# A decoder step with Strassen products: decode states through ScalarE and an adding transfer, and all 16 K tiles by Strassen in the heads and first convolutions

## The chip, the cores and the metric

The program runs on one core of one Trainium2 chip. The engines are TensorE (PE, with its weight loads shown apart as PEld), VectorE (DVE), ScalarE (ACT), GpSimd (POOL) and SyncE (SP). POOL and SP issue most transfers, each in the order of its own queue. The metric is the time of one execution on the device in microseconds; lower is better.

## The reference, cut to what matters

Two layers of a decoder trunk run over 512 prompt tokens and 8 single-token samples, which share all weights; all data is float32.

```
h = rmsnorm(x, norm_g);  z = h @ w_in            # 2048 -> 8192
b_c, c_c, x_c, g_c, q, k, v, g_r = split(z)      # 8 parts of 1024
y_conv = b_c * conv3(c_c * x_c) * silu(g_c)
q, k = rope(q), rope(k) / 16                     # 4 heads of 256
S_new = gamma * S + k^T v;  o = q S_new          # a sample: one step on its own state S (256 x 256)
y_ret = groupnorm(o) * gn_g * silu(g_r)          # the prompt: the same by chunks, from S = 0
x = x + concat(y_conv, y_ret) @ w_out
x = x + sigmoid(x @ w_pg) * (p @ w_ple)
```

Behind the last layer stands an RMSNorm. The new states of all samples and heads are outputs, with the retention decay gamma_h = 1 - 2^(-5-h).

## The kernel before

Activations lie transposed, 128 features by T = 520 tokens in a slot; there are 16 K tiles of 128 and NSLOT slots that are handed out and given back in program order. Tokens are two halves of TH = 260 (LEFT, RIGHT). A product of float32 accuracy is three matmuls of 128 x 128 by 128 x 260: `mm3` (L247 to L249) multiplies the high part of the weights by the high and the low part of the activation, and the low part of the weights by the high part.

Weights come from DRAM by SP into a ring of raw tiles (`raw_ring`) and are split by `split_w`: ScalarE writes the high part (L229), VectorE subtracts it to get the low part (L230). High and low go into `split_ring`, a ring of SPLIT tiles in pieces of up to four tiles (512 columns); a piece is free again when TensorE has used it.

`pair` makes two output tiles at a time. With s = 0 it is `plain`. With s > 0 the first s K tiles go through `strassen`: the pair's weights (two output tiles by two halves of the s tiles) and the activations (two halves of the tiles by the two halves of the tokens) are 2 x 2 blocks, and seven sets of s/2 products do what eight would. Each set's weights are sums made by VectorE (`add`, L319, pieces of up to four tiles); the sums of activations are made once per operand. The other 16 - s tiles follow plainly, two weight pieces and four products a tile. With s < 16 a fourth PSUM bank `c` is used and copied out at the end. The tables HEADS, CONVS, OUT_ROWS and GATES give s for each pair.

A layer is: four retention heads (`retain`), each of four pairs (q, k, v, gate); eight convolution steps of two pairs each; eight pairs with w_out; eight with w_pg. The prompt's retention runs in steps (`later`, called by `aside`) beside the pairs of the next head.

The decode step for a head h and a sample b runs in calls of `sample()`. A call comes at the end of every head's pair, and one more in the middle of every second; in the convolutions one in the middle of each pair, but for the last. A call first steps the sample that was loaded by the call ahead, then loads the next one: the state (`sret`, 256 KB, into slot `st`) and a row of key and query for all partitions (`kq`, into slot `kb`), both by POOL. The step (`sample_step`, L774) decays the state on ScalarE (L776), adds key times value on VectorE (L780, two of 256 columns, `vs` holds the values), sends the new state off (L781) and takes the dot products with the query (L784, two of 256 columns with an accumulator read each).

The order on each engine is set by the framework's scheduler, which may move instructions ahead within what data allows, by priorities; `keep(...)` holds an instruction in program order. Each engine then works its queue strictly in that order: one that waits holds up all behind it.

Of the kernel before, what the change touches and what calls it, by code (L numbers as in the profile page):

```python
# [13 lines left out]
P = 128  # L14
# [15 lines left out]
NSLOT = 75  # L30
# [22 lines left out]
HEADS = [[0, 0, 0, 8] + [14] * 12, [0] + [14] * 15]  # L53
CONVS = [[14] * 2 + [16] * 13 + [14]] * 2
# [10 lines left out]
SPLIT = 60  # L65
# [126 lines left out]
def trunk_kernel(  # L192
# [368 lines left out]
    vec = const.tile([P, 160], F32, name="vec")  # L561
# [17 lines left out]

    def gam(h):  # L580
        return vec[:, 128 + h : 129 + h]
# [93 lines left out]
    for a, b in ((0, 1), (1, 4), (4, 8), (8, 12), (12, 16)):  # L675
        raws = []
        if b == 1:
            raw = raw_ring.get(4)
            DMA.dma_start(raw.rearrange("p (m n) -> p m n", n=P), wi[0, 0:4, :, :P].rearrange("m p n -> p m n"))
            S.dma_start(vec, vecs)  # L680
            x = get()
            for n in (LEFT, RIGHT):
                DMA.dma_start(x[:, n], xT[0, :, n])
            xs.append(x)
            w = split_w(raw)
            ws = [[t[:, P * m : P * m + P] for t in w] for m in range(4)]
        else:
            for i in range(4):
                raws.append(load(wi[0, i, :, P * a : P * b]))
                if i < b - a:  # L690
                    x = get()
                    DMA.dma_start(x, xT[a + i])
                    xs.append(x)
            ws = [split_w(raw) for raw in raws]
            raw_ring.put(*raws)
# [20 lines left out]
    for l in range(DEPTH):  # L716
# [51 lines left out]
        def sample_load(h, b):  # L768
            st, kb = get(), get()
            SIDE.dma_start(st[:, :512], sret[l, h, b])  # L770
            SIDE.dma_start(kb[:, :512], kq[l, h, b].rearrange("c d -> (c d)").partition_broadcast(P))  # L771
            return h, b, st, kb

        def sample_step(h, b, st, kb):  # L774

            keep(S.activation(st[:, :512], st[:, :512], AF.Identity, scale=gam(h)))  # L776
            k = kb[:, 256:512]
            for e in range(2):
                c = slice(256 * e, 256 * e + 256)
                keep(V.scalar_tensor_tensor(st[:, c], k, vs[:, h, e, b : b + 1], st[:, c], MUL, ADD))  # L780
            SIDE.dma_start(o_rets[l, h, b], st[:, :512])  # L781
            for e in range(2):
                c = slice(256 * e, 256 * e + 256)
                V.tensor_tensor_reduce(k, st[:, c], kb[:, :256], 1.0, 0.0, MUL, ADD, osum[:, e, h, b : b + 1])  # L784
            put(st, kb)

        loaded = []

        def sample():

            if loaded:
                sample_step(*loaded.pop(0))
# [24 lines left out]
        def retain(h):  # L817
# [29 lines left out]
            for e, z in enumerate(head(mt + 4)):  # L847
                t = z.slot if z.ps is None else copied(z.ps).slot
                V.scalar_tensor_tensor(vs[:, h, e, :], t[:, SEQ:T], 1.0 / 16, rb[:, SEQ:T], MUL, MUL)
# [227 lines left out]
        for j in range(CJ):  # L1077
# [23 lines left out]
            if j == CJ - 1:  # L1101
                while loaded or todo:
                    sample()
# [375 lines left out]
```

## Time and profile before

| | |
|---|---|
| time, 3 runs | 2167.03, 2167.06, 2169.21 us; median 2167.06 |
| span of the profiled execution, first to last instruction | 2167.3 us |
| TensorE busy | 2147.8 us, 17861 matmuls, granted clock 0.999 |
| VectorE busy | 1896.1 us, 3849 instructions |
| ScalarE busy | 1264.5 us, 2647 instructions |
| GpSimd busy | 430.6 us, 746 instructions |
| moved by transfers | 387.31 MB, 179 GB/s on the mean |

The profiled execution's span lies within the three times, so a sum against the span holds for the times too. A row of a group gives the line, engine, operation, the tiles out<-in with their shapes, the count, then the busy time, the mean duration, and the idle time just before with what ended it. The busy time counts overlapped stretches once, so busy time over count is what one more costs, and the mean is how long one takes.

### The profile page before, as it was taken

The page shows a single profiled execution, that of the slowest core. Times are in us where ns is not written, and L with a number is a line of the kernel's source. Part 1 is how long each engine was busy: PE and PEld are TensorE (multiplying, and loading weights), DVE is VectorE, ACT ScalarE, POOL GpSimd, SP SyncE. Part 2 cuts the span into 40 slices and gives each one's busy share as a digit, 9 for nine tenths or more (in the row PEclk, how much of TensorE's full clock was granted, in tenths as well). Part 3 has the DMA queues.
Part 4 walks back from the last instruction along what each step waited for, and adds up shares of the span by engine and source line. Part 5 has one row for each costly group of instructions (what it writes and reads, how often), then busy time and mean ns, then how long its engine had stood idle before and what let it go on. Part 6 is the DMA issues. An engine that isn't in the chain of part 4 may idle for free. (4 is left out here: it accounts for less than half of the span.)

```text
span 2167.3 us, 48178 instructions
## 1 busy us (share of the span) xinstructions
PE 2147.8 (99%) x17861; PEld 2142.1 (99%) x17861; DVE 1896.1 (87%) x3849; ACT 1264.5 (58%) x2647; POOL 430.6 (20%) x746
## 2 busy tenths in 40 slices
PE   9999999999999999999999999999999999999998
PEld 9999999999999999999999999999999999999998
DVE  8889988998999987987997988989999998879884
ACT  8656655565555655655765655565645555456565
POOL 2313222211001211200212222231111022011011
PEclk9999999999999999999999999999999999999999
DMA  8555565545543745645645566664464355566455
GB/s 288 171 175 197 181 217 184 178 157 175 158 129 118 238 156 187 215 154 160 215 144 175 172 213 191 189 209 170 151 182 149 120 158 202 176 207 200 128 164 198
DMA packets 182861, 387.31 MB, mean 179 GB/s; under 512 B 25888, under 2 KB 56352, under 8 KB 182624
## 3 DMA queue, kind: packets, MB, share of 16 engines
q1 hardware_dynamic: 128704, 212.98, 31.6%
q0 software_dynamic: 53056, 169.84, 23.8%
q8 instruction: 140, 2.29, 0.4%
q10 hardware_dynamic: 864, 1.39, 0.2%
q14 instruction: 97, 0.79, 0.1%
HBM read 318.96 MB, written 65.15 MB: 177 GB/s over the span
## 5 line engine op out<-in xcount | busy, mean ns | idle before, releaser
L247 PE MATMUL ps_g<-slot,split 128*128 128x260 f32 x5465 | 1531.6, 284 | 7.2 <-ACT slot L307 2.9
L248 PE MATMUL ps_g<-slot,split 128*128 128x260 f32 x5465 | 1534.3, 282 | 0.3 <-DVE slot L555 0.3
L249 PE MATMUL ps_g<-slot,split 128*128 128x260 f32 x5461 | 1519.9, 283 | 0.5 <-DVE split L230 0.5
L229 ACT ACTIVATE split<-raw 128x512 fp32r<-128x512 f32 (+2 forms) x1347 | 777.3, 596 | 583.1 <-DVE raw L319 213.2
L247 PEld LDWEIGHTS ps_g<-slot,split 128*128 128x128 f32 x5465 | 1024.0, 188 | 10.1 <-ACT slot L307 3.7
L248 PEld LDWEIGHTS ps_g<-slot,split 128*128 128x128 f32 x5465 | 1028.5, 188 | 0.5 <-DVE slot L555 0.5
L249 PEld LDWEIGHTS ps_g<-slot,split 128*128 128x128 f32 x5461 | 1019.8, 188 | 1.0 <-DVE split L230 1.0
L230 DVE TENSOR_TENSOR split<-raw,split 128x512 fp32r<-128x512 f32 (+2 forms) x1346 | 849.2, 652 | 172.5 <-PE ps_g L248 85.4
L319 DVE TENSOR_TENSOR raw<-raw 128x512 f32<-128x512 f32 (+1 forms) x660 | 428.9, 660 | 32.5 <-DMA raw<-wi 23.7
L307 ACT ACTIVATE slot<-ps_g 128x260 f32<-128x260 f32 x336 | 127.4, 381 | 140.6 <-PE ps_g L249 122.7
L551 ACT ACTIVATE slot<-slot 128x520 fp32r<-128x520 f32 (+1 forms) x212 | 109.2, 562 | 46.6 <-DVE slot L414 11.1
L552 DVE TENSOR_TENSOR slot<-slot,slot 128x520 fp32r<-128x520 f32 (+1 forms) x212 | 124.4, 620 | 4.1 <-ACT slot L551 3.9
L781 POOL DMA_DIRECT2D o_rets<-slot x64 | 35.3, 552 | 351.6 <-DVE slot L780 131.7
L307 DVE TENSOR_TENSOR slot<-ps_g,slot 128x260 f32<-128x260 f32 x168 | 70.9, 424 | 6.0 <-PE ps_g L249 3.7
L869 POOL DMA_DIRECT2D slot<-hs x64 | 46.2, 724 | 118.7 <-DVE split L230 42.7
L814 POOL DMA_DIRECT2D hs<-slot x64 | 35.6, 556 | 139.3 <-DVE slot L755 61.3
L780 DVE SCALAR_TENSOR_TENSOR slot<-slot,vs,slot 128x256 f32<-128x256 f32 x128 | 56.1, 481 | 4.5 <-ACT slot L776 4.3
L746 DVE TENSOR_TENSOR slot<-slot,slot 128x520 f32<-128x520 f32 x80 | 55.8, 698 | 4.7 <-DMA o_rets<-slot 3.7
L770 POOL DMA_DIRECT2D slot<-sret x64 | 35.5, 554 | 114.6 <-ACT split L229 37.3
L1058 POOL DMA_DIRECT2D slot<-x1s x76 | 40.8, 538 | 87.6 <-PE ps_g L249 27.2
L1209 POOL DMA_DIRECT2D x2s<-slot x30 | 16.4, 545 | 201.6 <-DVE slot L1204 200.6
L771 POOL DMA_DIRECT2D slot<-kq x64 | 34.9, 547 | 106.0 <-DVE slot L876 22.2
(217 smaller groups left out, 1733.8 us busy)
## 6 DMA issues: line engine op xcount, KB each, us to landing
raw<-wi SPq DMA_DIRECT2D x377, 256.0 KB, 3.9
raw<-wo SPq DMA_DIRECT2D x128, 256.0 KB, 5.4
raw<-wg SPq DMA_DIRECT2D x122, 256.0 KB, 4.1
raw<-wi SPq DMA_DIRECT2D x136, 192.0 KB, 4.0
slot<-x1s POOLq DMA_DIRECT2D x76, 260.0 KB, 5.1
slot<-sret POOLq DMA_DIRECT2D x64, 256.0 KB, 4.0
hs<-slot POOLq DMA_DIRECT2D x64, 256.0 KB, 4.0
slot<-hs POOLq DMA_DIRECT2D x64, 256.0 KB, 5.2
```

What stands on the lines that cost most here:

```text
L229: S.activation(hi, raw, AF.Copy)
L230: V.tensor_tensor(lo, raw, F(hi), SUB)
L247: PE.matmul(out, wh, xh, start=start, stop=False, skip_group_check=more)
L248: PE.matmul(out, wh, xl, start=False, stop=False, skip_group_check=more)
L249: PE.matmul(out, wl, xh, start=False, stop=stop, skip_group_check=more)
L307: fn(*args)
L319: V.tensor_tensor(out[:, n], x[:, n], y[:, n], op)
L551: keep(S.activation(hi, src[:, n], AF.Copy))
L552: V.tensor_tensor(lo, src[:, n], F(hi), SUB)
L746: V.tensor_tensor(out[:, n], v, table[:, n], MUL)
L780: keep(V.scalar_tensor_tensor(st[:, c], k, vs[:, h, e, b : b + 1], st[:, c], MUL, ADD))
L869: SIDE.dma_start(t[:, :512].rearrange("p (m n) -> p m n", m=2), src)
```

## The change

The decode step is spread over three calls. A call steps one sample, prepares the next, and loads the key and query of the one after that. Preparing (`sample_add`) writes key times value into the state's slot on ScalarE, two instructions of 256 columns; then POOL sends the old state with `accum_op=ADD`, so that the transfer adds it to what lies there. The values in `vs` are divided by gamma, so the slot holds the new state over gamma. The step takes the dot products with GAMMA[h] as their scale, then ScalarE multiplies the state by GAMMA[h] and it is sent off. The dot products are now held in program order (`keep`), as is ScalarE's decay.

HEADS and CONVS go from 14 to 16 everywhere but in CONVS' last pair: 12 pairs of layer 0's heads, 15 of layer 1's, and the first two convolution pairs of each layer. NSLOT goes from 75 to 76, SPLIT from 60 to 56, and the constants `vec` from 160 to 128 columns.

```diff
-NSLOT = 75
+NSLOT = 76
...
+GAMMA = [1.0 - 2.0 ** (-5 - h) for h in range(H)]
+HEADS = [[0, 0, 0, 8] + [16] * 12, [0] + [16] * 15]
+CONVS = [[16] * 15 + [14]] * 2
-HEADS = [[0, 0, 0, 8] + [14] * 12, [0] + [14] * 15]
-CONVS = [[14] * 2 + [16] * 13 + [14]] * 2
...
-SPLIT = 60
+SPLIT = 56
...
         def sample_load(h, b):
-            st, kb = get(), get()
-            SIDE.dma_start(st[:, :512], sret[l, h, b])
+            kb = get()
             SIDE.dma_start(kb[:, :512], kq[l, h, b].rearrange("c d -> (c d)").partition_broadcast(P))
-            return h, b, st, kb
+            return h, b, kb
-        def sample_step(h, b, st, kb):
-            keep(S.activation(st[:, :512], st[:, :512], AF.Identity, scale=gam(h)))
-            k = kb[:, 256:512]
+        def sample_add(h, b, kb):
+            st = get()
             for e in range(2):
                 c = slice(256 * e, 256 * e + 256)
-                keep(V.scalar_tensor_tensor(st[:, c], k, vs[:, h, e, b : b + 1], st[:, c], MUL, ADD))
-            SIDE.dma_start(o_rets[l, h, b], st[:, :512])
+                keep(S.activation(st[:, c], kb[:, 256:512], AF.Copy, scale=vs[:, h, e, b : b + 1]))
+            SIDE.dma_start(st[:, :512], sret[l, h, b], accum_op=ADD)
+            return h, b, kb, st
+        def sample_step(h, b, kb, st):
             for e in range(2):
                 c = slice(256 * e, 256 * e + 256)
-                V.tensor_tensor_reduce(k, st[:, c], kb[:, :256], 1.0, 0.0, MUL, ADD, osum[:, e, h, b : b + 1])
+                keep(V.tensor_tensor_reduce(kb[:, 256:512], st[:, c], kb[:, :256], GAMMA[h], 0.0, MUL, ADD, osum[:, e, h, b : b + 1]))
+            keep(S.activation(st[:, :512], st[:, :512], AF.Copy, scale=GAMMA[h]))
+            SIDE.dma_start(o_rets[l, h, b], st[:, :512])
             put(st, kb)
-        loaded = []
+        loaded, added = [], []
         def sample():
+            if added:
+                sample_step(*added.pop(0))
             if loaded:
-                sample_step(*loaded.pop(0))
+                added.append(sample_add(*loaded.pop(0)))
             if todo:
                 loaded.append(sample_load(*todo.pop(0)))
...
-                V.scalar_tensor_tensor(vs[:, h, e, :], t[:, SEQ:T], 1.0 / 16, rb[:, SEQ:T], MUL, MUL)
+                V.scalar_tensor_tensor(vs[:, h, e, :], t[:, SEQ:T], 1.0 / 16 / GAMMA[h], rb[:, SEQ:T], MUL, MUL)
...
-                while loaded or todo:
+                while added or loaded or todo:
```

How this stands on the engines is shown at one call of `sample()`, the sixth, at the end of the pair for the second head's values in layer 0. Before, it steps the fifth sample of the first head; now it steps the fourth and prepares the fifth, which the next call steps, in the middle of the pair for the gate. Slots carry running numbers; what an instruction waits for stands in brackets (Activation is ScalarE, Pool GpSimd, DMASW a transfer of POOL's, DMAHW one of SP's). Lines of the new kernel are one to four off those of the old.

VectorE before: the fifth sample's two state updates (L780), then its dot products (L784) between weight splits (L230).

```order
L918 SCALAR_TENSOR_TENSOR slot_198_2369<-ps_kt,vec,slot_197_2368 128x256 [waits Activation_49]
L780 SCALAR_TENSOR_TENSOR slot_183_2055<-slot_184_2056,vs,slot_183_2055 128x256 [waits DMASW1_49,Activation_49]
L780 SCALAR_TENSOR_TENSOR slot_183_2055<-slot_184_2056,vs,slot_183_2055 128x256
L230 TENSOR_TENSOR split<-raw,split 128x512 [waits Activation_49]
L230 TENSOR_TENSOR split<-raw,split 128x512 [waits PE_49,Activation_49]
L784 ISA slot_184_2056,osum<-slot_183_2055,slot_184_2056 128x256 [waits DVE_49]
L784 ISA osum 128x1
L230 TENSOR_TENSOR split<-raw,split 128x256 [waits DMAHW4_49,PE_49,Activation_49]
L230 TENSOR_TENSOR split<-raw,split 128x256 [waits DMAHW6_49,Activation_49]
L784 ISA slot_184_2056,osum<-slot_183_2055,slot_184_2056 128x256 [waits DVE_49]
L784 ISA osum 128x1
L230 TENSOR_TENSOR split<-raw,split 128x384 [waits DMAHW2_49,PE_49,Activation_49]
```

VectorE after, from the second dot product of the fourth sample (L784, its accumulator read) to the first of the fifth, slot_199_2341:

```order
L784 ISA osum 128x1
L231 TENSOR_TENSOR split<-raw,split 128x512 [waits DMAHW6_49,PE_49,Activation_49]
L320 TENSOR_TENSOR raw<-raw 128x512 [waits DMAHW4_49,DVE_49]
L320 TENSOR_TENSOR raw<-raw 128x512 [waits DMAHW0_49,DVE_49]
L922 SCALAR_TENSOR_TENSOR slot_204_2494<-ps_vt,r5p,slot_203_2493 128x256 [waits DMASW4_49,Activation_49]
L231 TENSOR_TENSOR split<-raw,split 128x512 [waits DMAHW7_49,PE_49,Activation_49]
L231 TENSOR_TENSOR split<-raw,split 128x512 [waits PE_49,Activation_49]
L320 TENSOR_TENSOR raw<-raw 128x512 [waits DMAHW5_49,DVE_49]
L922 SCALAR_TENSOR_TENSOR slot_204_2494<-ps_vt,r5p,slot_203_2493 128x256 [waits Activation_49]
L308 TENSOR_TENSOR slot_202_2355<-ps_g,slot_202_2355 128x260 [waits DMASW6_49,Activation_49]
L320 TENSOR_TENSOR raw<-raw 128x512 [waits DVE_49]
L784 ISA slot_183_2029,osum<-slot_199_2341,slot_183_2029 128x256 [waits DMASW7_49]
```

The state updates are gone; the dot product of the fifth sample stands behind three splits (L231), four sums (L320) and three others, and waits for a transfer of POOL's.

ScalarE before, about the decay of the fifth sample (L776):

```order
L229 ACTIVATE split<-raw 128x384 [waits DMAHW6_49]
L917 ACTIVATE slot_197_2368<-ps_kt,vec 128x256 [waits DVE_49]
L776 ACTIVATE slot_183_2055<-slot_183_2055,vec 128x512 [waits DMASW0_49]
L229 ACTIVATE split<-raw 128x512 [waits DVE_49,Activation_49]
L229 ACTIVATE split<-raw 128x512 [waits DMAHW7_49,PE_49,Activation_49]
L229 ACTIVATE split<-raw 128x256 [waits DMAHW4_49,PE_49]
```

ScalarE after, from the decay of the fourth sample (L785, slot_182_2025) over the products of the fifth (L776) to the decay of the fifth:

```order
L785 ACTIVATE slot_182_2025<-slot_182_2025 128x512 [waits DMASW0_49,DVE_49]
L776 ACTIVATE slot_199_2341<-slot_183_2029,vs 128x256 [waits DMASW6_49]
L776 ACTIVATE slot_199_2341<-slot_183_2029,vs 128x256
L921 ACTIVATE slot_203_2493<-ps_vt,r5p 128x256 [waits PE_49]
L230 ACTIVATE split<-raw 128x512 [waits DMAHW7_49,PE_49]
L230 ACTIVATE split<-raw 128x512 [waits DVE_49,PE_49]
L921 ACTIVATE slot_203_2493<-ps_vt,r5p 128x256 [waits DVE_49]
L308 ACTIVATE slot_202_2355<-ps_g 128x260 [waits DMASW6_49,Activation_49]
L230 ACTIVATE split<-raw 128x512 [waits DMAHW3_49,PE_49]
L230 ACTIVATE split<-raw 128x512 [waits DVE_49,PE_49]
L785 ACTIVATE slot_199_2341<-slot_199_2341 128x512 [waits DMASW7_49,DVE_49,Activation_49]
```

The decay now waits for VectorE (its dot products), and the next sample's products stand right behind it, ahead of the next splits (L230).

POOL before: the sixth sample's state load (L770, slot_200_2382) stands four rows ahead of the fifth's new state going out (L781), and waits for nothing of the step.

```order
L770 DMA slot_200_2382<-sret 128x512 [waits PE_49]
L869 DMA slot_206_2526<-hs 128x2x256 [waits DMASW6_49,DMASW3_49]
L869 DMA slot_217_2960<-hs 128x2x256 [waits DMASW7_49,DVE_49,Pool_49]
L771 DMA slot_201_2383<-kq 128x512 [waits DMASW0_49,DVE_49]
L781 DMA o_rets<-slot_183_2055 128x512 [waits DMASW1_49,DVE_49,Activation_49]
L770 DMA slot_207_2560<-sret 128x512 [waits DMASW4_49,DMASW2_49,PE_49]
L781 DMA o_rets<-slot_200_2382 128x512 [waits DVE_49,Activation_49]
L771 DMA slot_208_2561<-kq 128x512 [waits DMASW3_49,DVE_49]
```

POOL after: the fifth sample's old state is sent (L777, slot_199_2341) right behind the fourth's new state (L786).

```order
L873 DMA slot_216_2899<-hs 128x2x256 [waits DMASW4_49,DVE_49,Pool_49]
L768 DMA slot_200_2345<-kq 128x512 [waits DMASW5_49,DVE_49]
L786 DMA o_rets<-slot_182_2025 128x512 [waits DMASW6_49,Activation_49]
L777 DMA slot_199_2341<-sret 128x512 [waits DMASW7_49,PE_49,Activation_49]
L786 DMA o_rets<-slot_199_2341 128x512 [waits DMASW0_49,Activation_49]
L777 DMA slot_206_2534<-sret 128x512 [waits DMASW2_49,PE_49,Activation_49]
L768 DMA slot_207_2538<-kq 128x512 [waits DMASW0_49,DVE_49]
```

A state's transfer stood some rows ahead of the step of the sample before it, and waited for its slot and for older transfers; now it stands behind that step's last transfer and waits for ScalarE's products too.

More of the change, by code (lines that the diff above doesn't have):

```diff
@@ L558, in split @@
         return op
-    vec = const.tile([P, 160], F32, name="vec")
+    vec = const.tile([P, P], F32, name="vec")
     def norm_g(l, k):
@@ L578, in kd @@
         return vec[:, c : c + 1]
-    def gam(h):
-        return vec[:, 128 + h : 129 + h]
     ident = const.tile([P, P], F32, name="ident")
@@ L679, in trunk_kernel @@
             DMA.dma_start(raw.rearrange("p (m n) -> p m n", n=P), wi[0, 0:4, :, :P].rearrange("m p n -> p m n"))
-            S.dma_start(vec, vecs)
+            S.dma_start(vec, vecs[:, :P])
             x = get()
```

## The prediction

> **What bounds the kernel now.** I read the page's busy table first, then the costliest groups, then the rate of matmuls in a quiet stretch. In the last row here the columns behind the stretch and its length are, for PE, the weight loads, DVE, ACT and POOL, the busy us and the number of instructions, then clock, DMA share and GB/s.
>
> ```profile
> span 2167.3 us, 48178 instructions
> PE 2147.8 (99%) x17861; PEld 2142.1 (99%) x17861; DVE 1896.1 (87%) x3849; ACT 1264.5 (58%) x2647; POOL 430.6 (20%) x746
> L247 PE MATMUL ps_g<-slot,split 128*128 128x260 f32 x5465 | 1531.6, 284 | 7.2 <-ACT slot L307 2.9
> 500.00:550.00 50.00, 50.00 (x420) 50.00 (x419) 44.04 (x89) 26.20 (x55) 8.75 (x15) 1.00 0.58 176
> ```
>
> TensorE is busy 99% of the span, and the costliest group shows 7.2 us of idle time in 1531.6. A group's "284 ns" overlaps its neighbours; what one matmul costs is the pace: 420 in 50 us, 119 ns each, at the full granted clock. The profiled execution's span is 2167.3 us; the three times given have the median 2167.06, so the sum below can be set against either.
>
> Where TensorE is not at that pace was read next, from its own waits and from stretches of 10 us (84 matmuls at full pace).
>
> ```profile
> PE ps_g L247 <- ACT slot L307: 2.9, 4, 1.3
> PE ps_g L247 <- ACT ps_g L307: 1.6, 2, 1.2
> PE ps_vt L913 <- DMA slot<-hs: 0.9, 1, 0.9
> ...
> 700.00:710.00 10.00, 8.80 (x73) 1.00 0.52 147
> 720.00:730.00 10.00, 7.88 (x64) 1.00 1.01 376
> 1780.00:1790.00 10.00, 8.71 (x73) 1.00 0.90 315
> 1790.00:1800.00 10.00, 9.44 (x79) 1.00 0.97 352
> ```
>
> The waits are small everywhere. The only sizable losses of pace are the two passages from the convolutions to w_out: 73, 64, 73 and 79 matmuls instead of 84 are 47 missing, 47 x 0.119 = 5.6 us, with the DMA engines at 0.52 to 1.01. So what shortens the program is fewer matmuls, as long as VectorE and ScalarE still deliver the split weights in time. How near VectorE is to its end shows by stage (the columns as above; the first four are layer 0's retention heads, then its convolutions, then two heads of layer 1):
>
> ```profile
> 87.00:168.00 81.00, 81.00 (x680) 81.00 (x679) 69.58 (x151) 46.89 (x101) 18.52 (x33) 1.00 0.57 188
> 168.00:253.40 85.40, 85.40 (x717) 85.40 (x716) 81.05 (x182) 51.47 (x115) 26.11 (x45) 1.00 0.63 199
> 253.40:346.30 92.90, 92.90 (x779) 92.90 (x778) 84.16 (x188) 55.37 (x123) 26.30 (x46) 1.00 0.66 207
> 346.30:410.00 63.70, 63.70 (x534) 63.63 (x533) 56.09 (x129) 38.53 (x87) 19.29 (x33) 1.00 0.55 178
> 410.00:700.00 290.00, 289.06 (x2415) 288.88 (x2414) 263.85 (x526) 158.92 (x320) 38.58 (x56) 1.00 0.48 149
> 1236.40:1322.90 86.50, 86.50 (x727) 86.50 (x727) 79.67 (x180) 51.85 (x116) 26.04 (x45) 1.00 0.62 195
> 1322.90:1417.70 94.80, 94.59 (x791) 94.39 (x791) 84.33 (x190) 55.49 (x124) 26.35 (x45) 1.00 0.65 199
> ```
>
> TensorE is busy to the last 0.01 us in the heads of layer 0, though VectorE works 81.05 of 85.40 us (95%) in one of them. That is the fact that I lean on most: the split ring is deep enough that a VectorE at 95% costs TensorE nothing.
>
> **TensorE's part of the change.** A pair of output tiles by s K tiles of Strassen takes 7s/2 + 4(16-s) products of three matmuls: 57 for s = 14, 56 for s = 16. Raised are 12 pairs of layer 0's heads, 15 of layer 1's, and two convolution pairs per layer: 31 pairs, 93 matmuls. 93 x 0.119 = 11.1 us off the path, the only term on it. [...]
>
> **VectorE's part.** Of the split groups, the pairs lose two pieces of 256 columns each (62), and seven splits and four sums of each grow from 384 to 512 (217 and 124). I price by busy time over count, since neighbours overlap.
>
> ```profile
> L230 DVE TENSOR_TENSOR split<-raw,split 128x512 fp32r<-128x512 f32 x1031 | 695.0, 690 | 147.8 <-PE ps_g L248 81.2 <-ACT split L229 51.8 <-issue 6.1
> L230 DVE TENSOR_TENSOR split<-raw,split 128x384 fp32r<-128x384 f32 x249 | 137.1, 555 | 16.2 <-ACT split L229 9.9 <-PE ps_g L248 3.4 <-ACT slot L551 1.9
> L230 DVE TENSOR_TENSOR split<-raw,split 128x256 fp32r<-128x256 f32 x66 | 27.3, 423 | 8.5 <-ACT split L229 7.6 <-PE ps_g L248 0.8
> L319 DVE TENSOR_TENSOR raw<-raw 128x512 f32<-128x512 f32 x520 | 354.1, 688 | 17.6 <-DMA raw<-wi 12.1 <-DMA raw<-wo 2.9
> L319 DVE TENSOR_TENSOR raw<-raw 128x384 f32<-128x384 f32 x140 | 77.4, 554 | 14.9 <-DMA raw<-wi 11.6 <-DMA raw<-wg 2.8
> L780 DVE SCALAR_TENSOR_TENSOR slot<-slot,vs,slot 128x256 f32<-128x256 f32 x128 | 56.1, 481 | 4.5 <-ACT slot L776 4.3
> ```
>
> One of 256 costs 0.414 us, so -62 x 0.414 = -25.6. A split grows from 137.1/249 = 0.551 to 695.0/1031 = 0.674: +217 x 0.123 = +26.8. A sum grows from 0.553 to 0.681: +124 x 0.128 = +15.9. That is +17.1 us, 0.55 a pair. The 128 state updates of the decode step leave: -56.1. Together -39 us; 1896 becomes about 1857. The dot products stay as they are, only their scale is another constant.
>
> **ScalarE's part.** It splits the same weights, saves one copy between banks in each of the 31 pairs (a fourth bank isn't used), and takes over the products of key and value.
>
> ```profile
> L229 ACT ACTIVATE split<-raw 128x512 fp32r<-128x512 f32 x1032 | 632.3, 626 | 462.3 <-DVE raw L319 188.2 <-PE ps_g L249 166.4 <-PE ps_g L248 45.1
> L229 ACT ACTIVATE split<-raw 128x384 fp32r<-128x384 f32 x249 | 127.2, 518 | 84.0 <-DVE raw L319 25.0 <-PE ps_g L248 24.2 <-PE ps_g L249 17.9
> L229 ACT ACTIVATE split<-raw 128x256 fp32r<-128x256 f32 x66 | 27.3, 415 | 36.7 <-DMA raw<-wi 29.0 <-PE ps_g L248 5.2 <-PE ps_g L249 1.9
> L307 ACT ACTIVATE ps_g<-ps_g 128x260 f32<-128x260 f32 x121 | 45.1, 373 | 16.4 <-PE ps_g L249 16.1
> L776 ACT ACTIVATE slot<-slot,vec 128x512 f32<-128x512 f32 x64 | 45.7, 714 | 0.0
> L917 ACT ACTIVATE slot<-ps_kt,vec 128x256 fp32r<-128x256 f32 x32 | 15.0, 468 | 9.2 <-DMA hs<-slot 3.2 <-DVE slot L918 2.5 <-PE ps_kt L913 2.2
> L874 ACT ACTIVATE slot<-slot 128x512 fp32r<-128x512 f32 x48 | 28.7, 624 | 10.1 <-DMA yc<-slot 4.6 <-DVE slot L904 2.4 <-DVE osum L784 2.1
> ```
>
> Splits: 217 x (0.613 - 0.511) - 62 x 0.414 = -3.5. Copies: -31 x 0.373 = -11.6. The 128 new products are 256 columns with a scale per partition, as in the row with ps_kt: 128 x 0.469 = +60.0. The 64 decays get a constant for a scale: 64 x (0.598 - 0.714) = -7.4. Together +37 us, 1264 to about 1302, 60% of the span: hidden, since no stage above has ScalarE over 61%. Were it not hidden, a head would show it as VectorE waiting for ScalarE's high halves.
>
> **The queues.** SP issues 62 transfers fewer for the same bytes (the two short pieces of each pair), worth nothing on the path. POOL issues as many as before, but the state's load now waits for ScalarE's products, and what stands behind it waits too: mostly the next kq row and the head's own fetches, needed a call later. The split ring shrinks from 60 to 56 tiles, 28 high and low pairs: 28 x 3 x 0.119 = 10.0 us of matmuls in stock instead of 10.7. I cost that at nothing; its cover is the stock itself. The 76th slot takes the room of those four tiles and of unused constants, and moves no work.
>
> **The new wait.** In the decode step a dot product now waits for a transfer that could not be sent before ScalarE wrote the products, and ScalarE writes them behind the decay of the sample ahead, which waits for that sample's dot products. So from one sample's dot products to the next one's there is a chain: decay, two products, transfer. All of VectorE's queue stands behind a dot product that waits, the weight splits above all, and TensorE behind those once the ring is empty. No row shows an adding transfer; the nearest is the plain load of the same 256 KB, whose 64 times from issue to landing (L770) are the first row.
>
> ```profile
> DMA to landing us min/median/max: 2.8/4.0/7.3
> ...
> L918 DVE SCALAR_TENSOR_TENSOR slot<-ps_vt,r5p,slot 128x256 fp32r<-128x256 f32 x32 | 15.4, 480 | 0.2 <-ACT slot L917 0.2
> L307 DVE TENSOR_TENSOR slot<-ps_g,slot 128x260 f32<-128x260 f32 x168 | 70.9, 424 | 6.0 <-PE ps_g L249 3.7 <-ACT slot L307 2.0
> ```
>
> By mean durations: 0.624 + 2 x 0.468 + 4.0 = 5.6 us if the adding transfer lands like the plain one. Against it stands the work that VectorE has between the two samples. At the place shown in the change's part it is three splits, four sums, two scaled subtractions (15.4/32 = 0.481) and one addition (70.9/168 = 0.422): 2.02 + 2.72 + 0.96 + 0.42 = 6.1 us. Added up so for all samples of a layer, five such gaps are 6.1 to 6.8 us (6.1, 6.1, 6.2, 6.8, 6.6), three 8.2 to 8.4, three 10.9 to 11.8, the others 13 and more. At 4.0 us nothing waits. The landing can hardly be shorter than the plain load's shortest, 2.8, which changes nothing, so the gain side of this term is zero. For the other end I double it, the state being read where it lands as well as where it comes from: 8.0, chain 9.6, and the dot products wait 16.2 us in the five gaps and 3.8 in the three, 20 us a layer. The idle time of VectorE in layer 0's four stretches of heads is 11.4 + 4.4 + 8.7 + 7.6 = 32.1 us; 20 samples fall there (20 x 2 x 0.438 = 17.5 us less work), 12 raised pairs (6.6 more) and 4.3 us less of TensorE's time leave 38.7. Twenty fit into 38.7, and one wait of 3.5 us is short against a stock of 10 us. I take the term as 0 on TensorE, nearer to the plain row, and keep 8 us as its upper end, from the second rival below.
>
> **Sum.** 2167.1 - 11.1 = 2156.0 us.
>
> **The rivals.**
> First, the adding transfer is so slow that the decode step's dot products stop VectorE: slower. It is decided where the waits of a layer pass the 38.7 us by half of 11.1 + 4.3 us, that is 46.4 us; with the gaps above that is a chain of 12.5, a landing of 10.9 us. At 12.0 us the waits are 52 + 8 = 60 us a layer, 21 more than the idle time, 43 for two layers: 2156 + 43 = 2199. [...] Against it: the plain load's longest landing of 64, with DMA shares of 0.57 to 0.66 around it, is 7.3 us. 7%.
> Second, the gain goes mostly back. With 8 us landing the close gaps come two by two: two waits of 3.5 us within 18 splits, whose 25 us of VectorE's work stand against 18 x 12 x 0.119 = 25.7 us of matmuls. VectorE falls 6 us behind there; if the ring is only half full, TensorE loses 1.3 us, three times a layer, and 8 us in all: 2164, no difference to be told. Against it is the 95% stretch. 12%.
> Third, the two passages lose less, as VectorE brings less backlog out of the convolutions (12 samples, 10.5 us less in 290): the 5.6 us go, 2150.5. Against it the DMA share of 1.01 in the worst stretch, which the change leaves. 15%.
> The forecast has the rest, 66%, with its own range of 2153 to 2159: 3 us either way for rearranged queues, about half of the passages' 5.6.
>
> **How the numbers follow.** A measurement of this kernel can tell a change from none at about 0.2%, 4.3 us. Faster: 66 + 15 = 81%; same, the second rival: 12%; slower, the first: 7%. The range leaves out the first rival and a part of the third: 2151 to 2164.
>
> **What will show it.** Right: TensorE's pace in the heads still 84 in 10 us with 93 matmuls fewer; VectorE's busy time near 1857, ScalarE's near 1302; the state's transfers landing within some 6 us, and hardly any idle time of VectorE before the dot products put down to them. Wrong: a row of VectorE's waits for the state's slot of tens of us, heads in which TensorE waits for split weights, a landing near 11 us, or a passage that loses clearly more than before.

## The result, and the profile after

The changed kernel takes 2202.4 us (2201.7 to 2203.1) where the kernel before takes 2167.5 in the same runs: 1.0161 times as long, interval 1.0147 to 1.0176. The forecast was 2156, with 2164 as its upper end. The first lines of the page, against those of before:

```profile
span 2201.0 us, 47885 instructions
PE 2152.6 (98%) x17768; PEld 2143.0 (97%) x17768; DVE 1877.6 (85%) x3659; ACT 1299.6 (59%) x2682; POOL 454.1 (21%) x746
```

The 93 matmuls are gone (17861 to 17768), and at the pace of 0.119 us a matmul that is 11.1 us. Two other things grew by more. TensorE's time without a matmul, span less busy time, was 2167.3 - 2147.8 = 19.5 us and is 2201.0 - 2152.6 = 48.4. Its busy time beyond the pace (called slow below), 2147.8 - 17861 x 0.119 = 22.3 before, is 2152.6 - 17768 x 0.119 = 38.2. So +28.9 idle, +15.9 slow, -11.1: together the 33.7 us between the two spans. What TensorE waited for, longest first, and what ScalarE's copies out of PSUM waited for:

```profile
PE ps_g L248 <- ACT slot L308: 17.4, 11, 3.9
PE ps_g L248 <- ACT split L230: 7.5, 6, 2.6
PE ps_g L250 <- DVE split L231: 3.7, 5, 1.7
```

```profile
ACT slot L308 <- DMA o_rets<-slot: 26.9, 12, 4.3
ACT slot L308 <- DMA hs<-slot: 6.3, 2, 3.5
```

L308 is the helper of `copy` and `plus` in `strassen`: ScalarE copies a bank into the pair's output slot, and TensorE cannot start the next product in that bank until it has. Before, such copies waited 2.8 us for `o_rets`; now 26.9. Most of the loss is in the retention heads (columns as in the prediction: PE, weight loads, VectorE, ScalarE, POOL, clock, DMA share, GB/s). The six stretches of heads held 4228 matmuls before and hold 3936 now; 292 at 0.119 us are 34.7 us of the 44.8. The convolutions run at full pace.

```profile
87.00:168.00 81.00, 79.06 (x650) 78.56 (x649) 71.36 (x137) 50.84 (x103) 17.82 (x27) 0.99 0.56 175
168.00:253.40 85.40, 84.38 (x698) 84.00 (x697) 73.14 (x149) 50.59 (x106) 24.23 (x40) 0.99 0.59 177
253.40:346.30 92.90, 86.99 (x704) 85.76 (x703) 74.67 (x154) 51.94 (x110) 28.19 (x45) 0.98 0.59 185
346.30:410.00 63.70, 61.26 (x506) 60.81 (x507) 55.33 (x113) 41.34 (x89) 19.23 (x31) 1.00 0.68 204
410.00:700.00 290.00, 290.00 (x2420) 290.00 (x2419) 262.26 (x510) 171.62 (x354) 45.30 (x69) 1.00 0.52 154
1236.40:1322.90 86.50, 80.50 (x654) 79.66 (x654) 69.33 (x141) 49.03 (x104) 24.48 (x40) 0.98 0.62 188
1322.90:1417.70 94.80, 89.29 (x724) 88.82 (x723) 79.07 (x163) 55.82 (x119) 27.31 (x44) 0.96 0.58 173
```

In the stretch at 253 us TensorE issues 704 matmuls where it issued 779, while VectorE is busy 75 of 93 us, less than before: no engine became the bound. One gap of it follows, first on ScalarE, then on POOL (start, duration, instruction, idle time before), then on TensorE by stretches (busy us and matmuls, clock, DMA share, GB/s):

```profile
254.96 0.62 ACT L785 ACTIVATE slot<-slot 128x512 f32<-128x512 f32 x1
...
259.17 0.63 ACT L230 ACTIVATE split<-raw 128x512 fp32r<-128x512 f32 x1 [1.40 <-PE ps_g L249]
264.06 0.67 ACT L308 ACTIVATE slot<-ps_g 128x260 f32<-128x260 f32 x2 [4.26 <-DMA o_rets<-slot]
```

```profile
255.58 2.14 POOL L873 DMA_DIRECT2D slot<-hs  x3 [3.17 <-ACT slot L785]
257.71 0.58 POOL L786 DMA_DIRECT2D o_rets<-slot  x1
```

```profile
258.00:261.00 3.00, 2.85 (x22) 1.00 0.76 210
261.00:265.00 4.00, 0.28 (x2) 1.00 1.06 347
265.00:268.00 3.00, 3.00 (x15) 0.50 0.49 162
268.00:271.00 3.00, 3.00 (x26) 0.94 0.00 0
```

The decay (L785), now the step's last work, ends at 255.6; the store of the new state is issued at 257.7, behind three fetches. The next pair's output has the same slot, so its copy stands still on ScalarE until 264.06, with the splits behind it, and TensorE has a gap of 3.72 us, from 261.06 to 264.78. Then the granted clock is 0.50 for 3 us, 15 matmuls where 25 fit. So the gap is paid nearly one and a half times. The clock record of the execution has six such stretches, each 3.41 us or twice that, 23.9 us in all; at half speed they lose 11.9 us, against 15.9 of slow time that came in. Before, there is none, but for one behind the last matmul, which both executions have. Ahead of the first of the six stands a gap of only 1.94 us, at 163.8.

### The profile page after: what moved, and what is told of

Read it like the earlier page. It is cut to its first block, busy times and chain, and to the rows that moved or that the text cites. A ratio compares the mean times of both kernels' runs of the same rounds, so it can differ in the third digit from the quotient of the medians.

```text
span 2201.0 us, 47885 instructions
## 1 busy us (share of the span) xinstructions
PE 2152.6 (98%) x17768; PEld 2143.0 (97%) x17768; DVE 1877.6 (85%) x3659; ACT 1299.6 (59%) x2682; POOL 454.1 (21%) x746
## 4 chain that ended last, share of the span: by engine, by line
PE 83%; DMA 6%; DVE 4%; issue 4%; ACT 2%; POOL 1%; SPq 0%; POOLq 0%; DVEq 0%; ACTq 0%
PE ps_g L248 26%; PE ps_g L250 26%; PE ps_g L249 26%; DMA raw<-wi 2%; DVE split L231 2%; DMA o_rets<-slot 1%; DMA hs<-slot 1%; DMA raw<-wo 1%; ACT split L230 1%; DMA slot<-sret 1%; DMA slot<-hs 1%; DVE raw L320 1%; PE ps_p L250 0%; PE ps_p L248 0%; PE ps_p L249 0%
## 5 line engine op out<-in xcount | busy, mean ns | idle before, releaser
L248 PE MATMUL ps_g<-slot,split 128*128 128x260 f32 x5434 | 1530.2, 285 | 27.5 <-ACT slot L308 17.4
L230 ACT ACTIVATE split<-raw 128x512 fp32r<-128x512 f32 (+1 forms) x1285 | 785.3, 624 | 675.6 <-PE ps_g L249 447.0
L231 DVE TENSOR_TENSOR split<-raw,split 128x512 fp32r<-128x512 f32 (+1 forms) x1284 | 851.3, 681 | 193.1 <-ACT split L230 173.1
L320 DVE TENSOR_TENSOR raw<-raw 128x512 f32<-128x512 f32 (+1 forms) x660 | 442.3, 680 | 10.6 <-DMA raw<-wi 5.6
L308 ACT ACTIVATE slot<-ps_g 128x260 f32<-128x260 f32 x336 | 124.0, 372 | 55.5 <-DMA o_rets<-slot 26.9
L786 POOL DMA_DIRECT2D o_rets<-slot x64 | 35.7, 558 | 492.1 <-ACT slot L785 458.6
L308 DVE TENSOR_TENSOR slot<-ps_g,slot 128x260 f32<-128x260 f32 x168 | 71.0, 423 | 25.0 <-ACT slot L308 15.6
L785 ACT ACTIVATE slot<-slot 128x512 f32<-128x512 f32 x64 | 40.0, 625 | 42.4 <-DVE osum L784 42.4
L784 DVE CUSTOM_DVE_ANT_0 slot<-slot,slot 128x256 f32<-128x256 f32 x128 | 53.3, 417 | 13.3 <-DMA slot<-sret 10.4
L777 POOL DMA_DIRECT2D slot<-sret x64 | 56.7, 887 | 19.1 <-ACT slot L776 12.0
```

What stands on the lines that cost most here:

```text
L230: S.activation(hi, raw, AF.Copy)
L231: V.tensor_tensor(lo, raw, F(hi), SUB)
L248: PE.matmul(out, wh, xh, start=start, stop=False, skip_group_check=more)
L308: fn(*args)
L320: V.tensor_tensor(out[:, n], x[:, n], y[:, n], op)
L777: SIDE.dma_start(st[:, :512], sret[l, h, b], accum_op=ADD)
```

## The experiments

Theory 1: the state's slot comes back late, because its store now stands behind the dot products. Theory 2: 16 instead of 14 asks more split weights of ScalarE and VectorE than they deliver in time. Theory 3, from the third group on: the ring of 56 holds too little stock. Theory 4: any edit lets the scheduler write another order on all engines, and the order of the kernel before is a favourable one. Ratios, with their 95% intervals, are to the kernel before on the same chip.

**The parts alone, and two cures for the slot.** The decode step alone:

```diff
 # the changed kernel, with the old tables
+HEADS = [[0, 0, 0, 8] + [14] * 12, [0] + [14] * 15]
+CONVS = [[14] * 2 + [16] * 13 + [14]] * 2
```

> The changed kernel with the old tables HEADS and CONVS (14): the new decode step and the new sizes alone, with the 93 matmuls back (17861). Theory 1, the state's slot comes back late because its store now ends the step, and copies out of PSUM that get this slot stall TensorE: the loss of 35 + 11 = 46 us stays whole, 2167 + 46 = 2213 us, with waits of ScalarE's L308 for the transfer that stores the state of 20 us or more in all. Theory 2, the longer Strassen in the heads asks more of the smaller split ring than it holds: the loss goes for the most part, 2167 to 2175 us. Half way, 2185 to 2195, would say that the two work together.

2189.0 us, 1.0091 (1.0076 to 1.0106): half way, which fits neither theory by itself. The 16 alone:

```diff
 # the kernel before, with the new tables
+HEADS = [[0, 0, 0, 8] + [16] * 12, [0] + [16] * 15]
+CONVS = [[16] * 15 + [14]] * 2
```

> The kernel before with HEADS and CONVS at 16 alone; ring of 60, 75 slots and the old decode step. Theory 1: the prediction's one term stands, 93 x 0.119 = 11.1 us less, 2156 us, pace 84 matmuls in 10 us in the heads. Theory 2: VectorE, 95% busy in one head already and with 17 us more work, runs late, and the time is 2175 to 2200 us, with TensorE's waits for split weights above 10 us in all.

2188.5 us, 1.0093 (1.0076 to 1.0110), though it has neither the new step nor the new sizes. Each part alone costs some 20 us against the kernel before on its chip. Own tiles for the states:

```diff
-NSLOT = 76
+NSLOT = 75
...
+    NST = 2
+    states = [const.tile([P, 512], F32, name=f"state{i}") for i in range(NST)]
...
-            st = get()
+            st = states[state_n[0] % NST]
+            state_n[0] += 1
...
-            put(st, kb)
+            put(kb)
```

> The changed kernel with the states in two tiles of their own, used in turn, and 75 slots for the rest: no copy out of PSUM can get the slot of a state that is still being stored. Theory 1: ScalarE's waits of L308 for the stored state (26.9 us in 12 waits) are gone, TensorE's wait for L308 falls from 17.4 us to under 5, and with the dips of the granted clock behind those gaps some 25 to 40 us come back: 2162 to 2178 us. Theory 2: the waits move to split weights and the time stays within 10 us of 2202. A load of a state that has to wait for the store of the state two samples ahead could cost something; it would show as waits of VectorE's L784 for the state's transfer above the 10.4 us of now.

2180.6 us, 1.0060 (1.0045 to 1.0075): 21.8 us come back, a little less than theory 1 said. The rows that it named:

```profile
PE ps_g L248 <- ACT slot L308: 5.8, 5, 1.9
PE ps_vt L921 <- DMA slot<-hs: 4.6, 4, 1.9
```

```profile
ACT slot L308 <- DMA hs<-slot: 6.9, 2, 3.6
```

No row of a copy that waits for a stored state is left, and TensorE's wait for L308 fell by 11.6 us. But 12 us above the kernel before on its chip, with 93 matmuls less, something else is still wrong. The same wait shortened in another way:

```diff
-            SIDE.dma_start(o_rets[l, h, b], st[:, :512])
+            S.dma_start(o_rets[l, h, b], st[:, :512])
```

> The changed kernel with one edit: the new state is sent off by ScalarE's own queue instead of POOL's, right behind the decay, so that it no longer stands behind three fetches of the next head on POOL (2.1 us at 255 us and at 1339 us). Theory 1: the slot is free about 2 us earlier in the worst places, gaps of 4.0 and 4.2 us become about 2: TensorE's wait for L308 falls from 17.4 us to about 8, and half of the loss comes back, 2180 to 2190 us. Theory 2: within 5 us of 2202. [...]

2201.9 us, 1.0150 (1.0132 to 1.0169): no change, and the wait is as long as it was:

```profile
ACT slot L308 <- DMA o_rets<-slot: 27.1, 12, 3.9
```

So what stands ahead of the store on POOL's queue is not what makes the wait; the three fetches at 255 us were one place, not the cause. Slots are held by the step's whole chain. In this run one dot product waits 2.82 us for its adding transfer at 1437 us, the second ends at 1443.0, and the copy behind it, which by its row waits for that dot product and for no store, makes TensorE's longest gap, 4.84 us:

```profile
1439.88 0.43 DVE L784 CUSTOM_DVE_ANT_0 slot<-slot,slot 128x256 f32<-128x256 f32 x1 [2.82 <-DMA slot<-sret]
1443.00 0.08 DVE L784 DVE_READ_ACCUMULATOR2_ANT osum<- 128x1 f32 x1
```

```profile
1443.12 0.39 ACT L308 ACTIVATE slot<-ps_g 128x260 f32<-128x260 f32 x1 [0.98 <-DVE osum L784]
```

**The sizes alone, a spare bank, one slot more.** The sizes:

```diff
 # the kernel before
-NSLOT = 75
+NSLOT = 76
-SPLIT = 60
+SPLIT = 56
...
-    vec = const.tile([P, 160], F32, name="vec")
+    vec = const.tile([P, 132], F32, name="vec")
...
-            S.dma_start(vec, vecs)
+            S.dma_start(vec, vecs[:, :132])
```

> The kernel before with the new sizes alone: ring of 56 tiles, 76 slots (and the constants' tile cut to the columns that are used). If four tiles fewer of split weights in stock matter, the time rises by 5 us or more, 2172 to 2180. If the prediction's zero for the ring holds, 2165 to 2170; the slot more could take some us of waits for slots away (18 us on ScalarE and VectorE in the kernel before, hardly any of it on TensorE).

2203.4 us, 1.0160 (1.0144 to 1.0177), above both ranges. Sizes that the prediction costed at nothing, with no work changed but a shorter load of constants, cost as much as the whole change. The spare bank:

```diff
-        c = banks.get() if s < KT else None
+        c = banks.get() if s < KT or spare[0] else None
```

(`spare[0]` is set during the pairs of the retention heads; the rest is the kernel before with the 16.)

> The kernel before with HEADS and CONVS at 16 (as the run that had them alone, 2188.5 us), but the pairs of the retention heads keep the fourth PSUM bank: the copy behind the second set of products goes to that bank, as with 14, and not into the output's slot. Theory 1, widened: with 16, a pair writes its output slot two sets (5 us) earlier, and ScalarE, which stands there until the slot's last transfer is out, holds up all splits behind it: ScalarE's waits of L307 for hs and o_rets transfers fall from 19 us to under 8, and the time goes to 2158 to 2175. Theory 2, the eighth K tile per set costs VectorE its quiet stretch at the end of a pair: no change, 2183 to 2193. The copies cost ScalarE 27 x 0.37 = 10 us more, hidden.

2183.7 us, 1.0071 (1.0056 to 1.0086), within what theory 2 said; the widened theory 1 falls. TensorE's wait for L308 went from 7.5 to 4.5 us, but its waits for ScalarE's splits from 8.7 to 13.2. Both cures together, the edits of the third and the sixth run:

> The changed kernel with both remedies: states in two tiles of their own and 75 slots (alone 2180.6 us), and the fourth PSUM bank kept in the pairs of the heads. Theory 1: both sources of waits for slots are gone, and the 93 matmuls show: 2156 to 2167 us. Theory 2: 2176 to 2186, as without the bank.

2185.6 us, 1.0091 (1.0067 to 1.0114): no better than the state tiles alone. One slot more in the changed kernel:

```diff
-NSLOT = 76
+NSLOT = 77
```

> The changed kernel with one more slot, 77, and nothing else. Theory 1: every slot rests one hand-out longer before it comes round again, some 2 to 5 us, so most of the waits of ScalarE's L308 for the stored state (26.9 us, the longest 4.3) go: 2175 to 2192 us. Theory 2: 2197 to 2207.

2188.9 us, 1.0093 (1.0078 to 1.0108), 13.5 less than with 76, in theory 1's range; the copies' waits for `o_rets` fell from 26.9 to 15.2 us. (A slot more moves the order too, as the next run shows, so not all of this need be the slot's.)

**Ring, slot or order.** One constant at a time in the kernel before, then an edit that changes no work, and the ring back in the changed kernel:

```diff
-NSLOT = 75
+NSLOT = 76
```

> The kernel before with 76 slots instead of 75 and nothing else; the ring stays at 60. Theory 3, the ring: the 34 us of the run with both sizes come from the four ring tiles, a slot more can only relax waits: 2163 to 2170 us. Theory 4, the order: any change of sizes lets the scheduler write another order on every engine (here 3754 lines of difference in 3274 rows of VectorE), and the order of the kernel before is a favourable one among many: 2180 to 2205 us although nothing was taken away.

```diff
-SPLIT = 60
+SPLIT = 56
```

> The kernel before with a split ring of 56 instead of 60 tiles and nothing else; 75 slots. Theory 3: the loss of the run with both sizes is here, 2195 to 2206 us. Theory 4: some other draw of the same kind, 2175 to 2205 us; it and the run with a slot more would both lose.

```diff
 # the kernel before
-            put(st, kb)
+            put(kb, st)
```

> The kernel before with one edit that changes no work and no size: the decode step gives its two slots back in the other order, put(kb, st) for put(st, kb). From there on other tiles stand in other slots, and the order on the engines changes (1266 lines of difference on VectorE, 776 on ScalarE). Theory 3: 2164 to 2171 us. Theory 4: clearly slower, 2175 us or more, with losses in the retention heads and the passages.

```diff
 # the changed kernel
-SPLIT = 56
+SPLIT = 60
```

> The changed kernel with the old ring of 60 tiles and 76 slots. Theory 3: nearly all of the loss goes, 2202 - 34 = 2168, and with the 11 us of the matmuls down to 2157; 2155 to 2172. Theory 4: another draw with no systematic gain, 2178 to 2205. Theory 1 (the state's slot) leaves it at 2190 to 2202 with ScalarE's waits of L308 for o_rets transfers of 20 us or more.

A slot more: 2185.7 us, 1.0087 (1.0070 to 1.0104). The smaller ring: 2189.7, 1.0104 (1.0088 to 1.0119). The null edit: 2167.2, 0.9996 (0.9987 to 1.0006). The changed kernel with 60: 2179.3, 1.0052 (1.0037 to 1.0067). The ring costs 22 us here and 23 there, which is theory 3's way, though both times lie outside its ranges and inside theory 4's. A slot more, which takes nothing away, costs 18, as theory 4 has it. The null edit is against theory 4, which had it slower; it moved the order less (by the two expectations, 1266 lines of difference on VectorE against 3754 for the slot). That tiles in other places make the instructions slower is not the reason: a matmul takes 284 ns on the mean in all three of before, the slot more and the smaller ring, and a split of 512 columns on VectorE 690, 685 and 684.

The smaller ring has a mark of its own, TensorE's waits for ScalarE's splits (before, then with 56):

```profile
PE ps_g L247 <- ACT split L229: 1.5, 2, 1.3
```

```profile
PE ps_g L247 <- ACT split L229: 9.3, 8, 3.3
```

In the changed kernel this row is 7.5 us with 56 and 0.6 with 60, though its waits for VectorE's splits go from 3.7 to 6.1. So a part of the ring's cost looks like stock that ran out, as theory 3 has it; but the decode step alone, also with 56, has only 0.7. Four more runs were to tell:

```diff
 # the changed kernel with SPLIT = 60
         def sample_step(h, b, kb, st):
+            keep(S.activation(st[:, :512], st[:, :512], AF.Copy, scale=GAMMA[h]))
+            SIDE.dma_start(o_rets[l, h, b], st[:, :512])
             for e in range(2):
                 c = slice(256 * e, 256 * e + 256)
-                keep(V.tensor_tensor_reduce(kb[:, 256:512], st[:, c], kb[:, :256], GAMMA[h], 0.0, MUL, ADD, osum[:, e, h, b : b + 1]))
-            keep(S.activation(st[:, :512], st[:, :512], AF.Copy, scale=GAMMA[h]))
-            SIDE.dma_start(o_rets[l, h, b], st[:, :512])
+                keep(V.tensor_tensor_reduce(kb[:, 256:512], st[:, c], kb[:, :256], 1.0, 0.0, MUL, ADD, osum[:, e, h, b : b + 1]))
```

> The changed kernel with the ring back at 60 (2179.3 us), and the decay and the new state's store put ahead of the dot products again, which then have the scale 1; the adding transfer, the pinned dot products and the 16 stay. Theory 1: the store goes out some 2 to 5 us earlier, ScalarE's waits of L308 for o_rets transfers (17.6 us in 10 waits with the ring at 60) fall to under 8 us, and the time to 2160 to 2172. If the late store costs nothing, 2176 to 2183. New risk: VectorE's dot products now wait for the landing and for ScalarE's decay behind it, 0.6 us more; with waits there above 20 us the time would be 2183 or more.

2167.8 us, 0.9995 (0.9986 to 1.0005): 11.5 us less than with the late store, as theory 1 said. The first two rows are of the run with the ring at 60 and the late store, the last three of this one:

```profile
PE ps_g L248 <- ACT slot L308: 11.5, 10, 3.2
...
ACT slot L308 <- DMA o_rets<-slot: 17.6, 10, 2.3
```

```profile
PE ps_g L248 <- ACT slot L308: 2.7, 3, 0.9
...
ACT slot L308 <- DMA o_rets<-slot: 5.1, 3, 2.5
...
ACT slot L781 <- DMA slot<-sret: 24.5, 14, 3.4
```

The copies' waits fell to 5.1 us and TensorE's for them by 8.8, about as much as lies between the two profiled spans (2176.5 and 2167.6). This edit too rewrites the order, so the 11.5 us are the store's as far as these rows show it. The wait for the adding transfer, now in front of the decay, is 24.5 us on ScalarE, and no row of TensorE's waits names it.

The decode step alone with that ring:

```diff
 # the changed kernel, with the old tables
-SPLIT = 56
+SPLIT = 60
```

> The changed kernel with HEADS and CONVS at 14 and the ring at 60: the new decode step alone, with 76 slots (2189.0 us with the ring at 56). If the ring costs some 22 us whatever else the kernel holds, as it did in the kernel before and in the changed one: 2164 to 2172. If the new decode step has a cost of its own through its late store: 2176 to 2190.

2194.9 us, 1.0111 (1.0089 to 1.0132), above both ranges: with 14, the larger ring is no faster than the smaller one (6 us slower by the medians, with intervals that overlap). So the ring does not cost 22 us whatever else there is. And beside the new decode step the 16 bring 2194.9 - 2179.3 = 15.6 us with the ring at 60, but cost 2202.4 - 2189.0 = 13.4 with the ring at 56 (medians from different chips; by the ratios 13 and 15); alone they cost 20.

The kernel before with a larger ring (the columns of constants cut as above, for room):

```diff
 # the kernel before
-SPLIT = 60
+SPLIT = 64
```

> The kernel before with a split ring of 64 tiles (and the unused columns of the constants cut for room). Theory 3, the stock in the ring: not slower than with 60, 2155 to 2169 us. Theory 4, the kernel before stands at a favourable order and any change of the ring's size leaves it: 2178 us or more.

2164.8 us, 0.9981 (0.9971 to 0.9990): a hair faster, within theory 3's range and against theory 4, which had 2178 or more. The last of the four:

```diff
 # the kernel before with NSLOT = 76, in each rule that counts free slots
-                if most and self.sent and len(slots.free) >= reserve + (7 if plain and summed else 3):
+                if most and self.sent and len(slots.free) - 1 >= reserve + (7 if plain and summed else 3):
```

> The kernel before with 76 slots (2185.7 us), but all three rules that count free slots, which decide when the next operand is prepared, take one off: the program is written in the order of the kernel with 75, and only each slot rests one hand-out longer. If the 18 us come from preparing operands earlier: 2164 to 2171. If they come from the scheduler's other order, as theory 4 says: 2178 to 2190.

2184.0 us, 1.0071 (1.0056 to 1.0086), as theory 4 had it. The program is written in the same order as with 75 slots; only tiles stand in other slots, and what the scheduler makes of it costs 15 us. Nine of them are in layer 0's heads, where the four stretches hold 77 matmuls fewer than before. The longest single gap is in a passage to w_out, where ScalarE's splits wait for transfers of weights, and TensorE behind them for the copy after the splits (ScalarE, then TensorE):

```profile
1801.52 0.63 ACT L229 ACTIVATE split<-raw 128x512 fp32r<-128x512 f32 x1 [2.65 <-DMA raw<-wo]
...
1804.54 0.63 ACT L229 ACTIVATE split<-raw 128x512 fp32r<-128x512 f32 x1 [1.18 <-DMA raw<-wo]
1806.48 0.63 ACT L229 ACTIVATE split<-raw 128x512 fp32r<-128x512 f32 x1 [1.32 <-DMA raw<-wo]
...
1807.55 0.37 ACT L307 ACTIVATE slot<-ps_g 128x260 f32<-128x260 f32 x1
```

```profile
1807.97 0.59 PE L247 MATMUL ps_g<-slot,split 128*128 128x260 f32 x1 [4.25 <-ACT slot L307]
```

Last, the ring at 64 in the early-store version (with room made by moving constants of the samples' norm into a slot and two small tiles to single buffers) and beside the 16 alone:

```diff
 # the changed kernel with the early store; the kernel before with the 16
-SPLIT = 60
+SPLIT = 64
```

> The changed kernel with the early decay and store (2167.8 us with a ring of 60) and a ring of 64; the room comes from constants of the samples' norm, which move into a slot, and from single instead of double buffers for two small tiles. If stock in the ring is what is short: 3 to 8 us less, 2158 to 2165, the first version of this family that is faster than the kernel before. If what is left are waits for slots and transfers: 2165 to 2172.

> The kernel before with HEADS and CONVS at 16 and a ring of 64 tiles; 75 slots and the old decode step. With the ring at 60 the 16 alone took 2188.5 us, 32 more than the 93 matmuls promise. If that is a shortage of stock: 2153 to 2172. If VectorE, which has 17 us more work and none taken away, or the slots are behind it: 2178 to 2190.

2180.3 us, 1.0054 (1.0041 to 1.0066), and 2193.3, 1.0115 (1.0099 to 1.0130). Both lie above every range that was given for them. The first is 12.5 us slower than with 60; the second, 4.8 slower by the medians with intervals that overlap, is at least no faster. Theory 3 falls as a rule. The losses of fourteen versions, worked out from the first lines of each page as above; the half clock is from the clock records, without the stretch behind the last matmul:

| version | time, us | idle | slow | of it half clock |
|---|---|---|---|---|
| before | 2167.5 | 19.5 | 22.3 | 0 |
| before, slots given back swapped | 2167.2 | 18.6 | 19.0 | 0 |
| before, ring 64 | 2164.8 | 16.5 | 21.7 | 1.7 |
| before, 76 slots | 2185.7 | 28.1 | 27.5 | 0 |
| before, 76 slots, old rules | 2184.0 | 28.0 | 28.5 | 5.1 |
| before, ring 56 | 2189.7 | 31.6 | 28.8 | 5.1 |
| before, 76 slots, ring 56 | 2203.4 | 35.3 | 37.4 | 10.2 |
| 16 alone, ring 60 | 2188.5 | 37.9 | 36.0 | 10.2 |
| decode step alone, ring 56 | 2189.0 | 29.1 | 28.9 | 1.7 |
| decode step alone, ring 60 | 2194.9 | 33.0 | 34.8 | 11.9 |
| changed | 2202.4 | 48.4 | 38.2 | 11.9 |
| changed, own state tiles | 2180.6 | 31.8 | 31.6 | 5.1 |
| changed, ring 60 | 2179.3 | 32.4 | 29.7 | 3.4 |
| changed, ring 60, early store | 2167.8 | 24.5 | 28.7 | 3.4 |

The first seven do the same work on every engine. Their times go from 2164.8 to 2203.4.

## Why the prediction was wrong

What engines do was forecast rightly. TensorE lost 93 matmuls; ScalarE came to 1299.6 us (forecast 1302); VectorE to 1877.6 (forecast 1857). Two prices of VectorE's were off: the 16 alone add 24.3 us (1920.4) where the prediction has 17.1, and the decode step alone takes 39.3 away (1856.8) where it has 56.1. The row of the state updates is gone with its whole 56.1 us; so busy time over count is not what one more costs the engine, as the method had it, but 39.3 / 128 = 0.31 us instead of 0.438. It counts overlap within its own group only, not with the neighbours. The adding transfer, the first rival's cause, is hardly slower than the plain load, and the dot products hardly wait for it:

```profile
slot<-sret POOLq DMA_DIRECT2D x64, 256.0 KB, 4.1
...
DVE slot L784 <- DMA slot<-sret: 10.4, 8, 3.5
```

So the first rival, though it gave 2199, is not what happened: that its time is near the measured one is chance. Nor did the second happen, which needed a landing of 8 us.

The step that failed is the sum: "the only term on it" for the matmuls, with "3 us either way for rearranged queues". What edits to sizes and to the release of slots do to the order and the waits was the largest term. Of the kernel before, six versions that change no work stand between -4 and +34 us of it on the same chip, four of them at +15 and more. That the order is what does it is argued, from the slot more and its run with the old rules; no run holds the order while the sizes change.

The prediction read "TensorE is busy to the last 0.01 us ... though VectorE works 81.05 of 85.40 us (95%)" as a property of a deep ring. The ring alone does not give it: with a slot more and the ring as it was, the same stretch reads (first row), while with the smaller ring and the slots as they were it keeps its full pace (second row):

```profile
168.00:253.40 85.40, 84.18 (x697) 83.43 (x696) 74.48 (x166) 48.10 (x106) 20.24 (x36) 1.00 0.57 181
...
168.00:253.40 85.40, 85.40 (x717) 85.40 (x716) 78.30 (x174) 50.93 (x113) 24.61 (x44) 1.00 0.61 192
```

Twenty matmuls fewer in the first, with VectorE at 87% instead of 95%. The smaller ring's loss lies elsewhere: the stretch of layer 1's heads at 1323 us holds 747 matmuls instead of 791.

Three terms stand inside it.

"I cost that at nothing; its cover is the stock itself", on the ring. In the changed kernel it measures 23.1 us (2202.4 to 2179.3), and TensorE's waits for ScalarE's splits fall by 6.9 with it (7.5 to 0.6). But it is no fixed price of four tiles of stock: the decode step alone gains nothing from them, and 64 tiles are slower than 60 in the early-store version.

The store. Under "The queues" the prediction followed the state's load past POOL's queue, and the new wait past VectorE's and ScalarE's. It never asked when the slot comes free. The decay and the store behind the dot products are part of the change, and who waits for them is the next owner of the slot. Moving them ahead again measures 11.5 us, and most of the rows of that wait go with it; own tiles measure 21.8 with the smaller ring. Both edits also rewrite the order.

The price of a wait. The prediction counts a matmul missed as 0.119 us. Behind the gap of 1.94 us at 163.8 stand 3.41 us at half clock, 1.7 us besides; in the changed kernel half clock is 11.9 us of the 45 lost.

The 16 were worth their 11 us in one pairing of four: 15.6 us beside the new decode step with the ring at 60. With the ring at 56 they cost 13.4 there, and alone, where VectorE keeps the state updates, 20 with a ring of 60 and 28.5 (2193.3 - 2164.8) with 64; a spare bank does not mend that either. Whether VectorE's load or the order does it was not separated. Also open are the last 12 us, from 2167.8 to 2156: idle 24.5 and slow 28.7 against 19.5 and 22.3 before, 11.4 us, of which half clock is 3.4; what makes the rest was not found. No version with the new decode step was faster than the kernel before; that kernel with a ring of 64 is, by 0.2%.

## What to carry to other kernels

Where a scheduler writes the order and the bound engine is busy 99%, the profile shows one order among many, here one of the better, and its zeros (waits, idle time) are no stock to spend. Before pricing an edit, run a few versions that change no work (a slot more, a smaller ring, a swapped release): their spread is a first measure of the error of a forecast there. For each step that is moved, follow the buffer to its next owner, past the last transfer that reads it. And count a gap on TensorE with the half clock that stands behind it in the trace: here 3.41 us at 0.50 behind 3.72 us without a matmul.

## What the hardware showed that I had not expected

The adding transfer of 256 KB lands in 4.1 us at the median, the plain one in 4.0; what it costs more is POOL's time to issue it, 885 ns against 544 (medians of 64). ScalarE's queue issues the same store in 338 ns (the run with the store on it), POOL in 550.

In the changed kernel's execution TensorE's granted clock goes to exactly 0.50 six times ahead of the last matmul, five times for 3.41 us and once for 6.83. The gaps on TensorE at these six starts are 1.94, 3.72, 2.60, 3.93, 2.79 and 1.32 us; the fourth, 1344.56 to 1348.49, still runs when the clock drops at 1346.99. Behind a gap of 3.16 us in the passage at 734 us, and one of 1.75 us at 1305, the clock stayed at 1.00 (the ends of matmuls in the profile are modelled). So the length of one gap does not tell whether half clock follows; what decides it was not shown.
